# The element-wise part of a long convolution beside attention: smaller steps, another share between two engines, and softmax sums finished in pairs

## The chip, the cores and the metric

One core of a Trainium2 chip runs the whole program in one launch. The metric is device time in microseconds: 3267.9, the median of three runs (3264.78 to 3273.39). The engines are TensorE (PE, with its weight loads as PEld), VectorE (DVE), ScalarE (ACT), GpSimd (POOL) and the DMA queues, of which SyncE (SP) issues most. Each engine has a queue of its own and works it off in order.

## The reference

Two layers of a trunk over 1024 latent tokens (x) and 256 context tokens, 1024 wide. Each layer norms and modulates its input, projects it, and feeds three mixers side by side: attention of 8 heads, a Fourier mixing and a long convolution. The output projection and a squared-ReLU MLP follow. In the second layer the context only gives keys and values. What the change touches is the softmax of the attention and the convolution by FFT:

```python
def block(qs):
    s = einsum('bqhd,bkhd->bhqk', qn, k_nope) + einsum('bqhr,bkr->bhqk', qr, k_rope)
    prob = jax.nn.softmax(s * scale, axis=-1)
    return einsum('bhqk,bkhd->bqhd', prob, v)
...
z = x1 * v
zf = jnp.fft.rfft(z, n=2 * L, axis=1)
kf = jnp.fft.rfft(k, n=2 * L, axis=0)
y = jnp.fft.irfft(zf * kf[None], n=2 * L, axis=1)[:, :L] + d_bias * z
return x0 * y
```

## The kernel before, in words

Every float32 product is made of three matmuls over a high and a low part (`mm3`, lines 138 to 140). The parts come from a copy on ScalarE and a subtraction on VectorE or GpSimd (`split_ps`, lines 143 and 144, from PSUM; `split_sb`, lines 147 and 148, in SBUF).

`attention` walks over 8 heads and, in each, over pairs of query tiles of 128 tokens (`q2`; 4 pairs, and in layer 0 a fifth for the context, which reads only the 256 context keys). For a pair it makes scores against the latent keys (`sx`, 1024 columns, one PSUM tile for each query tile) and the context keys (`se`, both tiles in one bank). Per tile follow: the maximum on VectorE (L1004; L1001 for both tiles' `se`), the bias of the exponential (L1005; L1007 for the context pair), two exponentials on ScalarE that also give their sums (L1008, L1010), the sum of the two sums (L1011) and its reciprocal (L1012; L1015 for the context pair) on VectorE, and the multiplication of the tile `p` by it on GpSimd (L1017). One pair later `turn` transposes `p` on TensorE (L1038, tail L1046), the result `pst` is split into `pt`, and `values` multiplies it with the values (L1056, L1057); `ot` (L1061, L1062) adds the halves. Scores are made two pairs ahead.

Beside it runs `side_job` as a generator: each call of `tick` (one per query tile) advances it by a rate, 0.88 turns in layer 0 and 0.72 in layer 1. Its `hyena_apply` transposes and transforms z on TensorE into `X` (L507, `psz`), then does the element-wise part for both halves `bt` of the frequencies: `zcb` (4 combinations of 512 columns, L535), `zf` (8 of 256, L543), the product with the filter's spectrum (`yf`, `ym`, L552 to L557, 1024 columns), `uq` (8 of 256, L569), `uu` (8 of 256, L577) and the splits `uhl`. Even-numbered combinations go to VectorE, odd ones to GpSimd. TensorE then transforms back (`psy`), and `dz` (L596, L598) is finished. In layer 0 a short second stream for the context follows, without the combinations.

The order in the queues isn't the order of these calls: a scheduler places the recorded instructions on each engine when the program is built. So a generator's step says when something is offered, and the order in the queue has to be read from the built program.

Of the kernel before, what the change touches and what calls it, by code (L numbers as in the profile page):

```python
# [47 lines left out]
def trunk(tc, a):  # L48
# [3 lines left out]
    with ExitStack() as top:  # L52
# [119 lines left out]
        def first_modulation(psp):  # L172
            """scale of the first norm of layer 0, both streams, on TensorE"""
# [36 lines left out]
        def rstd_diag(acc, n, dim, dg):  # L210
            """1 / sqrt(mean + eps) of each token, acc summed over its partitions, on diagonals of 128 tokens"""
# [10 lines left out]
        def rstd_rows(dg, n, r=None):  # L222
            """what rstd_diag found as rows, the same in every partition"""
# [23 lines left out]
        def norm_gen(l, i, xT, c0, c1, hs, acc, dg):  # L247
            """hi and lo parts hs of the modulated norm of tokens c0 to c1, acc filled by sums_by; dg is room"""
# [20 lines left out]
        def final_sums(acc, xs, ps):  # L269
            """as sums_by, the sums over the partitions in every row of ps"""  # L270
# [32 lines left out]
        def new_h(pool, chunks):  # L303
            """tiles for a norm's result: (start, end, hi and lo parts, what is still to run before their use)"""
# [11 lines left out]
        def sine_layers(pool, psp):  # L316
            """the filters' two sine layers, of both model layers and both lengths, to DRAM"""
# [27 lines left out]
        def filters(l, pool, psp):  # L345
            """the long filters' spectra of layer l, to DRAM"""
# [138 lines left out]
        def hyena_apply(l, stream, pool, psp):  # L485
# [35 lines left out]
            for ct in range(2):  # L521
# [4 lines left out]
                dz.append(dzt)  # L526
            Us = []
            for bt in range(2):
# [3 lines left out]
                else:  # L532
                    cb = b8("zcb").rearrange("p (k c f) -> p k c f", k=4, c=2)
                    for i, (p, q, op) in enumerate(((0, 2, ALU.add), (0, 2, ALU.subtract), (1, 3, ALU.add), (1, 3, ALU.subtract))):
                        (G if i % 2 else V).tensor_tensor(cb[:, i].rearrange("p c f -> p (c f)"), x[:, p].rearrange("p c f -> p (c f)"),  # L535
                                        x[:, q].rearrange("p c f -> p (c f)"), op=op)
                    yield
                    zf = b8("zf").rearrange("p (c f n) -> p c f n", c=2, f=4)
                    for c, f, i, ic, j, jc, op in ((0, 0, 0, 0, 2, 0, ALU.add), (0, 1, 0, 0, 2, 0, ALU.subtract),
                                                   (0, 2, 1, 0, 3, 1, ALU.subtract), (0, 3, 1, 0, 3, 1, ALU.add),  # L540
                                                   (1, 0, 0, 1, 2, 1, ALU.add), (1, 1, 2, 1, 0, 1, ALU.subtract),
                                                   (1, 2, 1, 1, 3, 0, ALU.add), (1, 3, 3, 0, 1, 1, ALU.subtract)):
# [10 lines left out]
                G.tensor_tensor(tc_, zs, ks, op=ALU.mult)  # L553
                V.tensor_tensor(yc, yc, tc_, op=ALU.subtract)
                G.tensor_tensor(ys, zc, ks, op=ALU.mult)
                G.tensor_tensor(ts_, zs, kc, op=ALU.mult)
                V.tensor_tensor(ys, ys, ts_, op=ALU.add)  # L557
# [5 lines left out]
                else:  # L563
                    y4 = y.rearrange("p (c f n) -> p c f n", c=2, f=4)
                    q = b8("uq").rearrange("p (k f) -> p k f", k=8)
                    for i, (c, f, g, op) in enumerate(((0, 0, 1, ALU.add), (0, 0, 1, ALU.subtract), (0, 2, 3, ALU.add),
                                                       (0, 3, 2, ALU.subtract), (1, 0, 1, ALU.subtract), (1, 0, 1, ALU.add),
                                                       (1, 2, 3, ALU.add), (1, 2, 3, ALU.subtract))):
                        (G if i % 2 else V).tensor_tensor(q[:, i, :], y4[:, c, f, :], y4[:, c, g, :], op=op)  # L569
                    A_, Ap, B_, H_, E_, Ep, D_, G_ = range(8)  # L570
                    yield
                    u = b8("uu").rearrange("p (r c f) -> p r c f", r=4, c=2)
                    for r, c, i, j, op in ((0, 0, A_, B_, ALU.add), (2, 0, A_, B_, ALU.subtract),
                                           (1, 0, Ap, D_, ALU.add), (3, 0, Ap, D_, ALU.subtract),
                                           (0, 1, E_, G_, ALU.add), (2, 1, E_, G_, ALU.subtract),
                                           (1, 1, Ep, H_, ALU.add), (3, 1, Ep, H_, ALU.subtract)):
                        (G if r % 2 else V).tensor_tensor(u[:, r, c, :], q[:, i, :], q[:, j, :], op=op)  # L577
                    yield
# [4 lines left out]
                yield  # L583
            for _ in range(3):
                yield
# [18 lines left out]
        def fnet(fs, pool, psp, with_ctx):  # L604
            """Fourier mixing, channels and then positions. Channels k of 1 to 31 of each group come with 64 - k, which hold
# [368 lines left out]
        def attention(l, heads, room, hpool, pools, psp, first):  # L974
# [5 lines left out]
            def scores(h, q2, i):  # L980
# [19 lines left out]
                if i == 0:  # L1000
                    V.reduce_max(sm, se, axis=AX.X)  # L1001
# [572 lines left out]
```

## Time and profile before

| what | value |
|---|---|
| median of three runs | 3267.9 us |
| profiled execution, first to last instruction | 3268.1 us |
| attention, layer 0 | about 396 to 772 us |
| attention, layer 1 | about 2081 to 2415 us |
| busy: PE, DVE, ACT, POOL | 95%, 56%, 37%, 32% |
| mean granted clock of TensorE | 0.978 |

The page gives no time around the span, so the span is taken as the profiled execution's own time. The two attention stages make up some 710 us of it; the rest is projections and MLP, with three matmuls per product one after another. A busy share is an average over a stretch: the table of stretches in the section of rows below shows the stages apart.

### The profile page before, as it was taken

Reading aid. Unit: us, or ns where it says so; the run is one execution under the profiler, and the core shown is the slowest. Engines: PE = TensorE matmul, PEld = TensorE weight load, DVE = VectorE, ACT = ScalarE, POOL = GpSimd, SP = SyncE. Lnnn points to the kernel's source line nnn. Section 1 sums busy time; section 2 is a strip of 40 time slices with the busy share of each in tenths; the row PEclk is TensorE's granted clock in tenths of the full one; section 3 lists DMA queues with packets and bytes.
Section 4 is the critical chain, followed back from the end, with each engine's and each line's share of the span. In section 5 each row is a group of like instructions: output and inputs, shape, how many; then the busy total and the mean of one; then the engine's idle time right before and its main releaser. Section 6 shows DMA issues by size and latency. Waiting matters only on the chain. (4 is left out here: it accounts for less than half of the span.)

```text
span 3268.1 us, 41676 instructions
## 1 busy us (share of the span) xinstructions
PE 3096.4 (95%) x16238; PEld 2584.0 (79%) x16238; DVE 1830.7 (56%) x2943; ACT 1204.9 (37%) x2167; POOL 1049.0 (32%) x676
## 2 busy tenths in 40 slices
PE   5999998999999999999999999998998999999997
PEld 1787886887778888888887887787877788888886
DVE  7985679886664444332226535779867322222226
ACT  4324475674331112112214424576654222222113
POOL 6334337542411111111113224347434222222223
PEclk8999998999999999999999998999999999999999
DMA  6454662434222232221113224653242111111113
GB/s 238 157 187 120 200 179 80 128 91 148 84 72 84 91 103 91 78 71 38 35 39 123 94 86 131 218 135 81 68 166 90 39 52 46 46 51 46 51 47 110
DMA packets 121036, 326.29 MB, mean 100 GB/s; under 512 B 32838, under 2 KB 44263, under 8 KB 120584
## 3 DMA queue, kind: packets, MB, share of 16 engines
q1 hardware_dynamic: 107832, 281.88, 27.7%
q0 software_dynamic: 9504, 34.67, 3.5%
q10 hardware_dynamic: 3504, 7.08, 0.6%
q8 instruction: 128, 2.10, 0.3%
q14 instruction: 68, 0.56, 0.1%
HBM read 270.11 MB, written 53.48 MB: 99 GB/s over the span
## 5 line engine op out<-in xcount | busy, mean ns | idle before, releaser
L134 POOL TENSOR_TENSOR wl<-wr,wh 128x1024 fp32r<-128x1024 f32 (+1 forms) x214 | 519.2, 2427 | 1641.8 <-ACT wh L133 1623.9
L133 ACT CAST wh<-wr 128x1024 fp32r<-128x1024 f32 (+1 forms) x214 | 221.5, 1035 | 962.0 <-PE pso L139 680.2
L140 PE MATMUL pso<-uh,wl 128*128 128x512 f32 (+1 forms) x1312 | 484.1, 369 | 4.2 <-POOL wl L134 4.2
L138 PE MATMUL pso<-uh,wh 128*128 128x512 f32 (+1 forms) x1312 | 487.5, 372 | 0.6 <-ACT wh L133 0.6
L1117 DVE SCALAR_TENSOR_TENSOR xT<-pso,modc,xT 128x512 f32<-128x512 f32 (+1 forms) x336 | 241.8, 722 | 438.4 <-PE pso L140 438.4
L138 PE MATMUL psm<-hh,wh 128*128 128x512 f32 (+1 forms) x1280 | 477.4, 374 | 4.3 <-ACT hh L244 4.2
L139 PE MATMUL pso<-ul,wh 128*128 128x512 f32 (+1 forms) x1312 | 480.7, 366 | 0.0
L140 PE MATMUL psm<-hh,wl 128*128 128x512 f32 (+1 forms) x1280 | 472.9, 370 | 3.5 <-POOL wl L134 3.5
L139 PE MATMUL psm<-hl,wh 128*128 128x512 f32 (+1 forms) x1280 | 474.9, 371 | 0.5 <-DVE hl L245 0.4
L1180 DVE SCALAR_TENSOR_TENSOR rl<-psm,rl 128x256 f32<-128x256 f32 (+1 forms) x160 | 101.7, 636 | 460.0 <-ACT rl L1179 459.9
L140 PEld LDWEIGHTS pso<-uh,wl 128*128 128x128 f32 x1312 | 247.8, 189 | 51.5 <-POOL wl L134 5.1
L139 PEld LDWEIGHTS pso<-ul,wh 128*128 128x128 f32 x1312 | 249.5, 190 | 45.2 <-issue 0.5
L138 PEld LDWEIGHTS pso<-uh,wh 128*128 128x128 f32 x1312 | 248.0, 189 | 44.5 <-ACT wh L133 0.8
L138 PEld LDWEIGHTS psm<-hh,wh 128*128 128x128 f32 x1280 | 241.7, 189 | 49.0 <-ACT hh L244 6.5
L140 PEld LDWEIGHTS psm<-hh,wl 128*128 128x128 f32 x1280 | 241.5, 189 | 47.9 <-POOL wl L134 3.9
L139 PEld LDWEIGHTS psm<-hl,wh 128*128 128x128 f32 x1280 | 241.6, 189 | 43.9 <-DVE hl L245 2.5
L1017 POOL TENSOR_SCALAR p<-p,st 128x1280 f32<-128x1280 f32 (+1 forms) x144 | 182.8, 1269 | 268.0 <-DVE st L1012 122.4
L144 DVE TENSOR_TENSOR pt<-pst,pt 128x512 fp32r<-128x512 f32 x328 | 214.4, 680 | 11.7 <-ACT pt L143 10.5
L143 ACT CAST pt<-pst 128x512 fp32r<-128x512 f32 x328 | 181.8, 589 | 86.3 <-PE pst L1038 68.2
L139 PE MATMUL psi<-hl,wh 128*128 128x512 f32 (+1 forms) x536 | 198.4, 370 | 5.8 <-POOL hl L241 3.4
L138 PE MATMUL psi<-hh,wh 128*128 128x512 f32 (+1 forms) x536 | 200.9, 376 | 1.8 <-ACT hh L244 1.1
L140 PE MATMUL psi<-hh,wl 128*128 128x512 f32 (+1 forms) x536 | 197.2, 368 | 3.2 <-POOL wl L134 3.2
(338 smaller groups left out, 6121.0 us busy)
## 6 DMA issues: line engine op xcount, KB each, us to landing
wr<-w SPq DMA_DIRECT2D x144, 512.0 KB, 3.5
wr<-wmod SPq DMA_DIRECT2D x64, 512.0 KB, 3.3
tb<-ftab POOLq DMA_DIRECT2D x34, 512.0 KB, 4.7
wm<-wmod SPq DMA_DIRECT2D x32, 512.0 KB, 3.6
wr<-wout SPq DMA_DIRECT2D x32, 512.0 KB, 3.6
wr<-win SPq DMA_DIRECT2D x26, 512.0 KB, 3.3
d_qk<-qk SPq DMA_DIRECT2D x18, 640.0 KB, 5.3
qk<-d_qk SPq DMA_DIRECT2D x18, 640.0 KB, 6.2
```

Of the source, the lines that this page charges most:

```text
L133: S.copy(hi[:, :n], t[:, :n])
L134: G.tensor_tensor(lo[:, :n], t[:, :n], hi[:, :n].bitcast(F32), op=ALU.subtract)
L138: T.matmul(ps, lhsT=lh, rhs=rh, start=first, stop=False)
L139: T.matmul(ps, lhsT=lh, rhs=rl, start=False, stop=False)
L140: T.matmul(ps, lhsT=ll, rhs=rh, start=False, stop=last)
L143: S.copy(hi, ps)
L144: V.tensor_tensor(lo, ps, hi.bitcast(F32), op=ALU.subtract)
L1017: G.tensor_scalar(pr, pr, st[:, 5:6], 1.0, op0=ALU.mult, op1=ALU.mult)
L1117: V.scalar_tensor_tensor(x, ps[:, : c1 - c0], g, x, op0=ALU.mult, op1=ALU.add)
L1180: V.scalar_tensor_tensor(r[:, :n], ps[:, :n], 0.0, r[:, :n], op0=ALU.max, op1=ALU.mult)
```

## The change

The generator's element-wise part yields after smaller pieces, and a helper `several` decides the engine: the first of every `per` combinations goes to VectorE, the others to GpSimd. `per` is 2 for `zcb` and 4 for `zf`, `uq` and `uu`. The product yields three times more. The order in which `uu` is listed changes. The waiting turns after the part go. The rates rise to 1.1 and 1.0. In the attention the maximum, bias and sums of a pair lie in two small tiles, and `normalise` adds and inverts both tiles' sums in one instruction each, after the second tile's exponentials; the two multiplications on GpSimd follow one another. Docstrings are dropped.

```diff
+            def several(ops, per):
+                for n, (o, x, y, op) in enumerate(ops):
+                    (V if n % per == 0 else G).tensor_tensor(o, x, y, op=op)
+                    if n % per == per - 1:
+                        yield
...
-                        (G if i % 2 else V).tensor_tensor(cb[:, i]..., x[:, p]..., x[:, q]..., op=op)
-                    yield
+                    yield from several([(flat(cb[:, i]), flat(x[:, p]), flat(x[:, q]), op) ...], 2)
...
-                        (G if f % 2 else V).tensor_tensor(zf[:, c, f, :], cb[:, i, ic, :], cb[:, j, jc, :], op=op)
+                    yield from several([(zf[:, c, f, :], cb[:, i, ic, :], cb[:, j, jc, :], op) ...], 4)
...
                 V.tensor_tensor(yc, zc, kc, op=ALU.mult)
                 G.tensor_tensor(tc_, zs, ks, op=ALU.mult)
+                yield
                 V.tensor_tensor(yc, yc, tc_, op=ALU.subtract)
                 G.tensor_tensor(ys, zc, ks, op=ALU.mult)
+                yield
                 G.tensor_tensor(ts_, zs, kc, op=ALU.mult)
+                yield
                 V.tensor_tensor(ys, ys, ts_, op=ALU.add)
...
-                        (G if i % 2 else V).tensor_tensor(q[:, i, :], y4[:, c, f, :], y4[:, c, g, :], op=op)
+                    yield from several([(q[:, i, :], y4[:, c, f, :], y4[:, c, g, :], op) ...], 4)
-                        (G if r % 2 else V).tensor_tensor(u[:, r, c, :], q[:, i, :], q[:, j, :], op=op)
+                    yield from several([(u[:, r, c, :], q[:, i, :], q[:, j, :], op) ...], 4)
...
                         split_sb(uh[:, r], ul[:, r], u[:, r], G)
+                        if r == 1:
+                            yield
                 Us.append((uh, ul))
-                yield
-            for _ in range(3):
                 yield
...
-                    V.tensor_tensor(st[:, 4:5], st[:, 2:3], st[:, 3:4], op=ALU.add)
-                    V.reciprocal(st[:, 5:6], st[:, 4:5])
-                G.tensor_scalar(pr, pr, st[:, 5:6], 1.0, op0=ALU.mult, op1=ALU.mult)
+            def normalise(p, q2):
+                s = p["s"]
+                if q2 < 4:
+                    V.tensor_tensor(s[:, :, 0], s[:, :, 0], s[:, :, 1], op=ALU.add)
+                V.reciprocal(s[:, :, 2], s[:, :, 0])
+                for i in range(2):
+                    G.tensor_scalar(p[i][1], p[i][1], s[:, i, 2:3], 1.0, op0=ALU.mult, op1=ALU.mult)
...
+                scores(pairs[n], h, q2, i)
                 tick()
+                exps(pairs[n], q2, i)
+                if i == 1:
+                    normalise(pairs[n], q2)
...
-                    spawn(0.72 if last else 0.88, side_job(l, psp, xctx, xT, rctx, raw))
+                    spawn(1.0 if last else 1.1, side_job(l, psp, xctx, xT, rctx, raw))
```

GpSimd's queue in layer 0, from the second product of the first half of the frequencies, before (`p` is a normalisation, `x2` two in a row):

```order
L556 TENSOR_TENSOR ym<-zf,wr 128x1024
L1017 TENSOR_SCALAR p<-p,st 128x1280
L148 TENSOR_TENSOR v<-wr,v 128x10x64
L569 TENSOR_TENSOR uq<-yf 128x256
L1017 TENSOR_SCALAR p<-p,st 128x1280
L569 TENSOR_TENSOR uq<-yf 128x256
L1017 TENSOR_SCALAR p<-p,st 128x1280
L569 TENSOR_TENSOR uq<-yf 128x256
L1017 TENSOR_SCALAR p<-p,st 128x1280
L569 TENSOR_TENSOR uq<-yf 128x256
L577 TENSOR_TENSOR uu<-uq 128x256 x4
L1017 TENSOR_SCALAR p<-p,st 128x1280
```

The same place after the change, from the context pair's two normalisations on (L530 is the line in `several`, L558 and L563 are the products, L1025 is the normalisation):

```order
L1025 TENSOR_SCALAR p<-p,st 128x256 x2
L558 TENSOR_TENSOR ym<-zf,wr 128x1024
L563 TENSOR_TENSOR ym<-zf,wr 128x1024
L310 DMA tb<-itab 128x1024
L530 TENSOR_TENSOR uq<-yf 128x256 x6
L530 TENSOR_TENSOR uu<-uq 128x256 x3
L1025 TENSOR_SCALAR p<-p,st 128x1280 x2
L530 TENSOR_TENSOR uu<-uq 128x256 x3
L148 TENSOR_TENSOR v<-wr,v 128x10x64
L1025 TENSOR_SCALAR p<-p,st 128x1280 x2
```

Normalisations, which stood singly between one or a few combinations, now stand in twos, with two products and nine combinations between one pair's and the next.

VectorE's queue in layer 0, from the last sum of the product on (L557), before:

```order
L557 TENSOR_TENSOR yf<-yf,ym 128x1024
L1012 RECIPROCAL st<-st 128x1
L144 TENSOR_TENSOR pt<-pst,pt 128x512
L1005 SCALAR_TENSOR_TENSOR st<-st,sm,acol 128x1
L144 TENSOR_TENSOR pt<-pst,pt 128x4x128
L569 TENSOR_TENSOR uq<-yf 128x256 x4
L1011 TENSOR_TENSOR st<-st 128x1
L1001 TENSOR_REDUCE sm<-se 128x2
L1012 RECIPROCAL st<-st 128x1
L1062 TENSOR_TENSOR ot<-ot,pv 64x256
```

The same place after the change (L565 is that sum; L1010 and L1004 are maxima, L1011 the bias, L1022 and L1023 the sum and the reciprocal for both tiles):

```order
L565 TENSOR_TENSOR yf<-yf,ym 128x1024
L1011 SCALAR_TENSOR_TENSOR sm<-sm,acol 128x1
L1069 TENSOR_TENSOR ot<-ot,pv 64x256
L1010 TENSOR_REDUCE sm<-sx 128x1
L1004 TENSOR_REDUCE sm<-se 128x2
L1022 TENSOR_TENSOR st<-st 128x2
L530 TENSOR_TENSOR uq<-yf 128x256
L1023 RECIPROCAL st<-st 128x2
L1011 SCALAR_TENSOR_TENSOR sm<-sm,acol 128x1
L144 TENSOR_TENSOR pt<-pst,pt 128x512
L1010 TENSOR_REDUCE sm<-sx 128x1
L530 TENSOR_TENSOR uq<-yf 128x256
```

Four `uq` in a row have become single ones among the attention's instructions, and one addition and one reciprocal serve both tiles of a pair.

## Rows read from the trace of the kernel before

**Rows 1.** The page's first part: busy us, share and instructions per engine.
```profile
PE 3096.4 (95%) x16238; PEld 2584.0 (79%) x16238; DVE 1830.7 (56%) x2943; ACT 1204.9 (37%) x2167; POOL 1049.0 (32%) x676
```

**Rows 2.** Stretches: length, busy us (instructions) of PE, PEld, DVE, ACT, POOL; clock, DMA.
```profile
493.00:594.30 101.30, 80.21 (x459) 69.00 (x458) 95.02 (x155) 56.83 (x121) 74.56 (x63) 0.85 0.26 67
690.00:760.00 70.00, 64.30 (x441) 56.01 (x440) 56.81 (x125) 51.92 (x114) 27.64 (x22) 1.00 0.48 158
2100.00:2201.00 101.00, 97.58 (x696) 88.19 (x695) 77.91 (x163) 77.26 (x161) 41.65 (x38) 1.00 0.52 134
2201.80:2317.60 115.80, 100.31 (x639) 85.06 (x638) 110.95 (x195) 79.50 (x167) 79.07 (x61) 0.96 0.29 72
```

**Rows 3.** Waits of TensorE, 493 to 594.3 us: total us, times, longest.
```profile
PE pv L1056 <- DVE pt L144: 7.4, 6, 2.9
```

**Rows 4.** Groups of VectorE, 493 to 594.3 us: busy us, mean ns | idle before.
```profile
L1005 DVE SCALAR_TENSOR_TENSOR st<-st,sm,acol 128x1 f32<-128x1 f32 x14 | 10.7, 766 | 0.1
L543 DVE TENSOR_TENSOR zf<-zcb 128x256 f32<-128x256 f32 x8 | 7.6, 984 | 0.1
L569 DVE TENSOR_TENSOR uq<-yf 128x256 f32<-128x256 f32 x8 | 6.8, 908 | 0.0
...
L1011 DVE TENSOR_TENSOR st<-st 128x1 f32<-128x1 f32 x15 | 5.7, 383 | 0.1
...
L577 DVE TENSOR_TENSOR uu<-uq 128x256 f32<-128x256 f32 x8 | 4.2, 567 | 0.0
...
L1012 DVE RECIPROCAL st<-st 128x1 f32<-128x1 f32 x15 | 2.2, 149 | 0.0
```

**Rows 5.** Groups of VectorE, 2201.8 to 2317.6 us.
```profile
L1005 DVE SCALAR_TENSOR_TENSOR st<-st,sm,acol 128x1 f32<-128x1 f32 x22 | 12.0, 547 | 0.0
L1011 DVE TENSOR_TENSOR st<-st 128x1 f32<-128x1 f32 x23 | 10.3, 449 | 2.7 <-ACT p L1010 2.5
...
L543 DVE TENSOR_TENSOR zf<-zcb 128x256 f32<-128x256 f32 x5 | 5.2, 1073 | 0.0
L577 DVE TENSOR_TENSOR uu<-uq 128x256 f32<-128x256 f32 x8 | 4.9, 646 | 0.0
...
L569 DVE TENSOR_TENSOR uq<-yf 128x256 f32<-128x256 f32 x8 | 4.5, 576 | 0.0
```

**Rows 6.** Groups of VectorE, 690 to 760 us (calm).
```profile
L1005 DVE SCALAR_TENSOR_TENSOR st<-st,sm,acol 128x1 f32<-128x1 f32 x15 | 4.2, 279 | 0.0
...
L1012 DVE RECIPROCAL st<-st 128x1 f32<-128x1 f32 x16 | 2.5, 156 | 0.1
L1011 DVE TENSOR_TENSOR st<-st 128x1 f32<-128x1 f32 x16 | 2.4, 152 | 4.5 <-ACT p L1010 4.4
```

**Rows 7.** Groups of GpSimd, 493 to 594.3 us.
```profile
L543 POOL TENSOR_TENSOR zf<-zcb 128x256 f32<-128x256 f32 x8 | 7.4, 951 | 0.1
L569 POOL TENSOR_TENSOR uq<-yf 128x256 f32<-128x256 f32 x8 | 6.9, 877 | 8.1 <-DVE st L1012 5.7 <-DVE st L1011 2.4
L577 POOL TENSOR_TENSOR uu<-uq 128x256 f32<-128x256 f32 x8 | 6.4, 819 | 1.1 <-DVE st L1011 1.1
L556 POOL TENSOR_TENSOR ym<-zf,wr 128x1024 f32<-128x1024 f32 x2 | 4.7, 2373 | 0.0
```

**Rows 8.** Timeline of VectorE: start us, us, engine, line, instruction.
```profile
499.83 1.92 DVE L1005 SCALAR_TENSOR_TENSOR st<-st,sm,acol 128x1 f32<-128x1 f32 x1
```

**Rows 9.** Timeline of GpSimd at the same time.
```profile
499.38 2.35 POOL L555 TENSOR_TENSOR yf<-zf,wr 128x1024 f32<-128x1024 f32 x1
```

**Rows 10.** Timeline of GpSimd, 2117 to 2125 us (calm).
```profile
2118.74 1.33 POOL L1017 TENSOR_SCALAR p<-p,st 128x1280 f32<-128x1280 f32 x1 [3.83 <-DVE st L1012]
2122.30 1.33 POOL L1017 TENSOR_SCALAR p<-p,st 128x1280 f32<-128x1280 f32 x1 [2.22 <-DVE st L1012]
```

**Rows 11.** Timeline of TensorE, the transposes of the first of these tiles.
```profile
2128.32 1.03 PE L1038 MATMUL pst<-ident,p 128*128 128x128 f32 x8
```

**Rows 12.** Waits of the whole run: VectorE's additions for an exponential's sum.
```profile
DVE st L1011 <- ACT p L1010: 59.8, 41, 4.0
```

More of the change, by code (lines that the diff above doesn't have):

```diff
@@ L581, in hyena_apply @@
                         split_sb(uh[:, r], ul[:, r], u[:, r], G)
+                        if r == 1:
+                            yield
                 Us.append((uh, ul))
-                yield
-            for _ in range(3):
                 yield
@@ L1009, in scores @@
-                if isx:
-                    S.activation(P[:, :SEQ], sx, AF.Exp, bias=st[:, 1:2], scale=ac, accum_out=st[:, 3:4])
-                    V.tensor_tensor(st[:, 4:5], st[:, 2:3], st[:, 3:4], op=ALU.add)
-                    V.reciprocal(st[:, 5:6], st[:, 4:5])
-                    pr = P
-                else:
-                    V.reciprocal(st[:, 5:6], st[:, 2:3])
-                    pr = P[:, SEQ:TT]
-                G.tensor_scalar(pr, pr, st[:, 5:6], 1.0, op0=ALU.mult, op1=ALU.mult)
@@ L1018, in scores @@
-                yield P
+                me, mx, b = (m[:, 2 * u + i : 2 * u + i + 1] for u in range(3))
+                if q2 < 4:
+                    V.reduce_max(mx, p["x", i], axis=AX.X)
+                    V.scalar_tensor_tensor(b, mx, me, nac, op0=ALU.max, op1=ALU.mult)
+                else:
+                    V.tensor_tensor(b, me, nac, op=ALU.mult)
+                S.activation(P[:, SEQ:TT], p["e"][:, i, :], AF.Exp, bias=b, scale=ac, accum_out=s[:, i, 0:1])
+                if q2 < 4:
+                    S.activation(P[:, :SEQ], p["x", i], AF.Exp, bias=b, scale=ac, accum_out=s[:, i, 1:2])
@@ L1063, in values, with emit @@
                 nc.sync.dma_start(out=d_cat[h // 2][mine, q2 * 256 : q2 * 256 + 256], in_=ot[mine])
-            units = [(h, q2, i) for h in range(HEADS) for q2 in range(nq2) for i in range(2)]
-            ready = {}
-            def emit_scores(n):
-                if n >= len(units):
+            todo = [(h, q2) for h in range(HEADS) for q2 in range(nq2)]
+            pairs = [{} for _ in todo]
+            def emit(n, i):
+                if n >= len(todo):
                     return
-                h, q2, i = units[n]
+                h, q2 = todo[n]
                 if q2 == 1 and i == 0 and h + 1 < HEADS:
@@ L1075, in emit_scores @@
                     split_v(h + 1, heads)
-                g = scores(h, q2, i)
-                next(g)
-                pending.append((n, g))
+                scores(pairs[n], h, q2, i)
                 tick()
-            pending = []
-            def softmaxes():
-                while pending:
-                    n, g = pending.pop(0)
-                    ready[n] = next(g)
+                exps(pairs[n], q2, i)
+                if i == 1:
+                    normalise(pairs[n], q2)
             for _ in range(2):
                 next(first)
-            for n in range(4):
-                emit_scores(n)
-                softmaxes()
-                if n == 1:
+            for n in range(2):
+                for i in range(2):
+                    emit(n, i)
+                if n == 0:
                     split_v(0, heads)
@@ L1096, in attention @@
                     spawn(1.0, first)
-            prev = []
-            for n in range(0, len(units), 2):
-                h, q2, _ = units[n]
+            for n, (h, q2) in enumerate(todo):
+                P = [pairs[n][i][0] for i in range(2)]
                 dst = [ptile(4) for _ in range(2)] if q2 < 4 else []
-                turn(ready[n], 0, dst)
-                emit_scores(n + 4)
-                softmaxes()
-                turn(ready[n + 1], 1, dst)
-                tail = turn_tail([ready.pop(n), ready.pop(n + 1)])
-                emit_scores(n + 5)
-                softmaxes()
+                turn(P[0], 0, dst)
+                emit(n + 2, 0)
+                turn(P[1], 1, dst)
+                tail = turn_tail(P)
+                emit(n + 2, 1)
                 pts = [(4 * b + u, dst[b][0][:, u], dst[b][1][:, u]) for b in range(len(dst)) for u in range(4)]
```

60 lines of the change are left out of this document (27 added, 33 removed).

## Prediction

> **What bounds the kernel now.** I read the page's table of engines first: TensorE is busy for 95% of the span, VectorE for 56%, GpSimd for 32% [rows 1]. An average like that hides stages, so next came the busy time by stretch [rows 2]. All that the change touches runs during the attention of the two layers, and there two stretches stand out. From 493.0 to 594.3 us (layer 0; called A) and from 2201.8 to 2317.6 us (layer 1; called B) the long convolution's element-wise part runs. In A VectorE is busy 95.02 of 101.30 us, TensorE only 80.21, at a granted clock of 0.85; in B VectorE 110.95 of 115.80, TensorE 100.31, at 0.96. In the two calm stretches beside them TensorE is idle 5.7 of 70 us and 3.4 of 101 us at full clock. So in A and B VectorE is the bound, elsewhere TensorE. The waits of TensorE in A agree: the longest one in total is for the second half of the split of transposed probabilities, which VectorE does late [rows 3].
>
> How much is there to win? Matmuls issued are a fair measure of progress, since the mix is nearly the same: 441 in the 70 us of the layer 0 calm stretch, that is 6.30 a us. A's 459 matmuls would take 72.9 us at that pace, B's 639 would take 101.4: 28.4 and 14.4 us are lost, 42.8 together. By the pace of the other calm stretch (696 in 101 us, more short ones) B loses 23.1. So 43 to 52 us is the most that mending A and B can give.
>
> **The change, part by part.**
>
> *Twelve 256-wide combinations per layer go from VectorE to GpSimd.* Before, each of three groups (zf, uq, uu) has eight, four on either engine, for two halves of the frequencies: 24 on VectorE. Now two of eight stay: 12 leave VectorE. In A the three groups hold eight each at 984, 908 and 567 ns [rows 4]; four of each are 4 x (0.984 + 0.908 + 0.567) = 9.8 us. In B they take 1073, 576 and 646 ns [rows 5], so 4 x 2.295 = 9.2 us. The zcb group and the products keep their engines. These durations hold waiting time (next point but one), so they are what VectorE gets back only if the waiting goes as well.
>
> *Sums finished for two query tiles together.* Per pair of tiles with all 1280 keys, one addition and one reciprocal go. The new ones are two elements wide instead of one; no row shows that width. It lies between free and twice the price of the 128x1 ones, which cost 152 and 156 ns when nothing disturbs them [rows 6]; twice would be 0.31 us a pair, 6 us in A and B together. I take free, since 152 ns for a single element is nearly all fixed cost. In A the addition takes 383 and the reciprocal 149 ns [rows 4]; with 7.5 pairs that is 4.0 us. In B it is (0.449 + 0.149) x 11 = 6.6 us [rows 4, 5]. Outside A and B about 52 pairs save 0.31 us each [rows 6], 16 us of VectorE; TensorE is the bound there, so between 0 and 16 of it shows. I take 4, near the low end, since TensorE's idle share in the calm stretches is only 3 to 8%.
>
> *What GpSimd gains.* It takes 12 more combinations per layer: in A at the mean of 951, 877 and 819 ns, 10.6 us more on a queue that is busy 74.56 of 101.30 us [rows 2, 7]. That is where the price is. A VectorE instruction with one element per partition (L1005, the bias of the exponential) took 1.92 us at 499.83 and ended together with GpSimd's multiplication yf, which ran from 499.38 for 2.35 us [rows 8, 9]. Its mean is 766 ns in A, 547 in B and 279 in the calm stretch [rows 4 to 6], while the reciprocal, which reads one tensor, stays at 149 to 156. The Trainium skill ("SBUF — State Buffer", section "Who interferes with whom") states this as a rule: a VectorE instruction with two SBUF inputs contends with a GpSimd instruction that reads SBUF, and whichever starts first blocks the other for the whole instruction. The trace agrees, 1.92 us against 0.28. By that rule taken whole, every combination handed to GpSimd becomes a lock of its own, and the sum is that of rival 1; by the price below, it is the forecast's.
>
> Price: in A the excess of L1005 is 14 x (0.766 - 0.279) = 6.8 us, that of the half of L1011 that remains 7.5 x (0.383 - 0.152) = 1.7. GpSimd's share would rise from 0.74 to (74.6 + 10.6) / 91 = 0.94, by a factor 1.27, so 2.3 us are added. The element-wise instructions left on VectorE pay a like sum (estimate: the same again), 4.5 in all. In B: 5.9 + 3.3 = 9.2 us of excess, share 0.68 to 0.84, 2.2 added, doubled 4.4. Bounds: nothing added (the instructions at risk are also fewer), or each of the 12 moved instructions blocks VectorE for its whole 0.7 to 0.9 us, 10 us a layer.
>
> *Normalisation later.* The first tile's multiplication now waits for the second tile's sums. In a calm place of layer 1 the two multiplications stand at 2118.74 and 2122.30, and the first tile is transposed from 2128.32 (the layer's ninth multiplication and ninth group of eight transposes) [rows 10, 11]. So the delay of 3.6 us eats into a lead of 8.25 and leaves 4.7: hidden. In the first pair of each layer there is hardly a lead; I charge 1 us for both. In A the cover is thin. In GpSimd's queue two multiplications ym, six uq and three uu now stand between one pair's normalisation and the next: 2 x 2.37 + 6 x 0.88 + 3 x 0.82 = 12.5 us [rows 7], against a pair's 8 to 9 in calm. Before, one or two combinations stood between normalisations there.
>
> *Small steps, higher rates, fewer waiting turns.* The generator now yields some 28 times where it yielded 15, at a rate of 1.1 for 0.88 (1.0 for 0.72 in layer 1). But in the finished order the part still spans nine or ten pairs on GpSimd's queue in layer 0 (8.5 before) and ten in layer 1 (11 before): it is not spread out. What the steps do is break up bursts of four uq or uu on VectorE. I count nothing for that. TensorE's inverse transforms move a few pairs later; their work is the same, and they lie in stretches where TensorE is the bound: 0. The loads on SP's queue shift with the steps, and none is on TensorE's path in A or B: 0.
>
> **Sum.** A: 9.8 + 4.0 - 4.5 = 9.3 us. B: 9.2 + 6.6 - 4.4 = 11.4. Outside 4, start -1. Together 24 us off the profiled execution's 3268.1 (0.2 above the median of the timed runs): 3244. After that VectorE is at about 86 of 92 us in A: still the bound, so the relief shows in full; GpSimd is close behind.
>
> **Rivals.**
> 1. GpSimd takes VectorE's place. For: the 12.5 us piece, a share of 0.94 in A, and L1005 held until yf ends. Against: GpSimd idles 26.7 us in A now, 8.1 of it before uq alone, waiting for VectorE [rows 7]. If each of the 24 moved instructions blocks VectorE for as long as it runs (10.6 + 8.8 us), 19.0 of element-wise relief becomes nothing; 10.6 of sums remain, less 5 for normalisations that come late: 3262.
> 2. The whole loss goes. For: once VectorE falls below TensorE, idling and the lower clock (0.85 in A) go together. Against: VectorE stays the longer one in A by my sum. 43 to 52 us: 3221.
> 3. Slower: the one sum left blocks VectorE's queue. In the whole run VectorE waits 59.8 us in 41 places for an exponential's sum before an addition [rows 12], 1.46 each, with reductions and splits queued behind. There are now 64 additions, each behind the later of two exponentials. If all 64 wait for 1.46 us, that is 93, or 34 more, and if TensorE feels it all, 24 won turn into 10 lost: 3278. It decides from 1.46 us per addition on. Against: the addition now comes once a pair, so there are half as many chances, and in calm stretches VectorE has slack.
>
> **How the numbers follow.** The forecast, 12 to 36 us won (3232 to 3256), gets 0.53; rival 1 (0 to 12 won) 0.21; rival 2 (over 36) 0.15; rival 3 and anything else that loses 0.11. Less than 0.3% (9.8 us) is about what a measurement can't tell from no change. Faster by more: 0.53 + 0.15 + a little of rival 1 = 0.70; same 0.20; slower 0.10. The range 3218 to 3270 leaves out the far end of rival 2 and most of rival 3.
>
> **What would show it.** Right: in the element-wise stretches VectorE's share falls below 94%, TensorE's clock comes back near 1.00, pairs take some 10% less; zf, uq and uu on VectorE 12 per layer; 64 additions and 72 reciprocals. Wrong: L1005's successor above 0.8 us with the stretches as long as now (rival 1); TensorE's transposes waiting for GpSimd's p (rival 1); VectorE waiting over 90 us for exponentials (rival 3); or gains in calm stretches, where I expect next to none.

## The result and the profile after

| kernel | median us | range | runs | ratio to before |
|---|---|---|---|---|
| before | 3267.99 | 3264.78 to 3274.76 | 5 | |
| changed | 3287.99 | 3282.57 to 3302.93 | 5 | 1.0066 [1.0048, 1.0084] |

The change makes the kernel slower by 20 us, 0.66%. The forecast was 24 us faster, so sign and range are both wrong. The execution that was profiled is the slowest of the five (span 3301.0 us; the others reach down to 3280.6), so it is read by progress inside a stretch (matmuls issued in it), not by its end.

The engine table of the page after, against [rows 1]: VectorE has 160 instructions less and 10.2 us less work, GpSimd 24 more and 23.8 us more, TensorE the same.

```profile
PE 3096.2 (94%) x16238; PEld 2581.6 (78%) x16238; DVE 1820.5 (55%) x2783; ACT 1205.7 (37%) x2167; POOL 1072.8 (32%) x700
```

Where the time goes is in the stretches. First three of the kernel before, cut by content this time: the whole element-wise part of layer 0 (from the first `zcb` to the last `uhl`), that of layer 1, and 100 us that hold the inverse transforms of layer 0. Columns as in [rows 2].

```profile
480.70:588.20 107.50, 88.37 (x532) 76.73 (x530) 100.38 (x162) 62.33 (x131) 77.05 (x65) 0.87 0.35 87
2178.80:2305.90 127.10, 112.42 (x740) 97.60 (x740) 120.79 (x211) 86.81 (x181) 88.31 (x73) 0.96 0.36 87
600.00:700.00 100.00, 96.21 (x668) 86.00 (x667) 80.25 (x167) 69.24 (x148) 49.61 (x48) 0.98 0.50 132
```

The same three after the change:

```profile
479.20:586.60 107.40, 83.92 (x531) 72.90 (x529) 89.36 (x134) 65.05 (x138) 85.31 (x78) 0.90 0.37 89
2186.60:2308.70 122.10, 104.83 (x677) 91.23 (x675) 111.09 (x161) 81.41 (x169) 94.86 (x81) 0.93 0.34 84
620.00:720.00 100.00, 86.15 (x582) 78.15 (x581) 65.23 (x122) 56.03 (x119) 41.77 (x43) 0.93 0.47 120
```

Three findings. In layer 0 VectorE has 11.0 us less to do (9.3 were forecast), and nothing comes of it: 531 matmuls in 107.4 us against 532 in 107.5. VectorE now idles 18 us where it idled 7. In layer 1, 677 matmuls at the pace of before (740 in 127.1) would take 116.3 us; they take 122.1: 5.8 lost. In the inverse transforms, 582 at the pace of before (668 in 100) would take 87.1; they take 100: 12.9 lost. Together that is 18.7 us, an estimate from matmul counts. Whole attentions of the same execution, from the first score matmul to the last `ot`, took 395.0 us instead of 375.6 in layer 0 and 340.4 instead of 337.1 in layer 1, so part of layer 1's 5.8 is won back outside its stretch. Of the 32.9 us that this span is longer than the one before, 8.8 lie ahead of the first attention, which the change doesn't touch.

The relief in layer 0 turns into this. VectorE in the changed kernel (start, us, line; L557 and L560 are the product and the subtraction of `yf`):

```profile
493.17 1.74 DVE L557 TENSOR_TENSOR yf<-zf,wr 128x1024 f32<-128x1024 f32 x1 [1.32 <-POOL zf L530]
501.76 3.35 DVE L560 TENSOR_TENSOR yf<-yf,ym 128x1024 f32<-128x1024 f32 x1 [6.84 <-POOL ym L558]
505.14 0.42 DVE L1069 TENSOR_TENSOR ot<-ot,pv 64x256 f32<-64x256 f32 x1
```

GpSimd at the same time:

```profile
490.45 5.76 POOL L530 TENSOR_TENSOR zf<-zcb 128x256 f32<-128x256 f32 x6
496.18 2.33 POOL L561 TENSOR_TENSOR yf<-zf,wr 128x1024 f32<-128x1024 f32 x1
498.49 0.93 POOL L1025 TENSOR_SCALAR p<-p,st 128x256 f32<-128x256 f32 x2
499.40 2.33 POOL L558 TENSOR_TENSOR ym<-zf,wr 128x1024 f32<-128x1024 f32 x1
501.69 2.33 POOL L563 TENSOR_TENSOR ym<-zf,wr 128x1024 f32<-128x1024 f32 x1
```

And TensorE:

```profile
505.71 1.94 PE L1045 MATMUL pst<-ident,p 128*128 128x128 f32 x8 [9.44 <-DVE ot L1069]
```

VectorE wants `ym`, which stands behind six `zf` in a row, another product and two normalisations: 6.84 us of waiting. Then the subtraction itself takes 3.35 us instead of 1.2, since GpSimd starts the next `ym` 0.07 us ahead of it. The `ot` behind it comes late, and TensorE stands for 9.44 us. Much of the price that the forecast spread over many instructions is paid in one place. In the group means of the whole element-wise part of layer 0, against [rows 4], the bias is better than before (463 ns, it was 766). The paired addition is not: 767 ns where a single one took 383, so eight cost 6.1 us where fifteen cost 5.7. Over the whole run its median is 161 ns (152 in [rows 6] for the single one), so it isn't the second element that costs.

```profile
L1011 DVE SCALAR_TENSOR_TENSOR sm<-sm,acol 128x1 f32<-128x1 f32 x15 | 6.9, 463 | 0.0
L1022 DVE TENSOR_TENSOR st<-st 128x2 f32<-128x2 f32 x8 | 6.1, 767 | 2.1 <-ACT p L1016 2.0
...
L560 DVE TENSOR_TENSOR yf<-yf,ym 128x1024 f32<-128x1024 f32 x2 | 4.5, 2273 | 6.8 <-POOL ym L558 6.8
```

In layer 1 the same place shows another face. One bias of 128x1 lasts 7.16 us:

```profile
2209.45 7.16 DVE L1011 SCALAR_TENSOR_TENSOR sm<-sm,acol 128x1 f32<-128x1 f32 x1
```

GpSimd runs without a gap until 2216.59, 0.02 us before that bias ends:

```profile
2207.86 2.63 POOL L1025 TENSOR_SCALAR p<-p,st 128x1280 f32<-128x1280 f32 x2
2210.47 1.53 POOL L148 TENSOR_TENSOR v<-wr,v 128x640 fp32r<-128x640 f32 x1
2211.97 2.33 POOL L558 TENSOR_TENSOR ym<-zf,wr 128x1024 f32<-128x1024 f32 x1
2214.26 2.33 POOL L561 TENSOR_TENSOR yf<-zf,wr 128x1024 f32<-128x1024 f32 x1
```

In the inverse transforms it is a table, a block of coefficients that each group of matmuls needs. TensorE's waits from 600 to 720 us (us in all, times, longest), the first matmuls behind the longest wait, and the stretches ahead of it and behind it:

```profile
PE psy L138 <- DMA tb<-itab: 6.9, 3, 3.9
...
643.99 0.58 PE L138 MATMUL psy<-tb,uhl 128*128 128x256 f32 x1 [3.91 <-DMA tb<-itab]
644.37 0.41 PE L139 MATMUL psy<-tb,uhl 128*128 128x256 f32 x1
644.58 0.41 PE L140 MATMUL psy<-tb,uhl 128*128 128x256 f32 x1
...
630.00:640.00 10.00, 9.74 (x77) 8.86 (x76) 7.28 (x17) 6.74 (x16) 6.22 (x7) 1.00 0.50 119
644.00:648.00 4.00, 4.00 (x19) 4.00 (x19) 0.70 (x1) 0.00 (x0) 1.17 (x1) 0.50 0.12 39
```

After the idle 3.9 us the matmuls start 0.21 us apart where those ahead of the wait (from 638.41) started 0.12 apart. The granted clock is 0.50 from 644 to 648 us, the lower of its two levels (1.2 of 2.4 GHz), so the wait is paid a second time. The tables are requested from GpSimd's queue. The one of the longest wait was requested at 637.07, directly behind two normalisations, and TensorE went on 6.9 us later. Ahead of the next requests GpSimd's queue stood for 4.39 us until TensorE gave a buffer back:

```profile
634.48 2.67 POOL L1025 TENSOR_SCALAR p<-p,st 128x1280 f32<-128x1280 f32 x2 [1.47 <-DVE st L1023]
637.07 0.60 POOL L310 DMA_DIRECT2D tb<-itab  x1
...
652.02 1.25 POOL L310 DMA_DIRECT2D tb<-itab  x2 [4.39 <-PE psy L140]
```

### The profile page after: what moved, and what is told of

The parts are those of the page before. It is cut to its first block, busy times and chain, and to the rows that moved or that the text cites. A ratio compares the mean times of both kernels' runs of the same rounds, so it can differ in the third digit from the quotient of the medians.

```text
span 3301.0 us, 41509 instructions
## 1 busy us (share of the span) xinstructions
PE 3096.2 (94%) x16238; PEld 2581.6 (78%) x16238; DVE 1820.5 (55%) x2783; ACT 1205.7 (37%) x2167; POOL 1072.8 (32%) x700
## 4 chain that ended last, share of the span: by engine, by line
PE 71%; DVE 15%; ACT 4%; POOL 4%; issue 3%; DMA 2%; SPq 0%; ACTq 0%; POOLq 0%; DVEq 0%
PE pso L138 9%; PE pso L140 9%; PE pso L139 9%; PE psm L138 8%; PE psm L139 8%; PE psm L140 8%; DVE pt L144 3%; PE psi L138 3%; PE psi L140 3%; PE psi L139 3%; DVE sm L1010 2%; PE pv L1063 1%; PE pv L1064 1%; ACT p L1016 1%; DVE crow L201 1%
## 5 line engine op out<-in xcount | busy, mean ns | idle before, releaser
L1025 POOL TENSOR_SCALAR p<-p,st 128x1280 f32<-128x1280 f32 (+1 forms) x144 | 180.4, 1264 | 269.6 <-DVE st L1023 198.4
```

The lines of the kernel that those rows point to most:

```text
L1025: G.tensor_scalar(p[i][1], p[i][1], s[:, i, 2:3], 1.0, op0=ALU.mult, op1=ALU.mult)
```

## The experiments

All ratios are to the kernel before; each variant was timed 5 to 12 times. Three theories: the split makes VectorE and the normalisations wait for GpSimd (1); the sums for two tiles bring the normalisation late (2); the steps and the rate move the inverse transforms to where they collide (3).

**One part at a time.** `c_pair_only` is before with the paired sums, `a_split_only` before with three of four combinations on GpSimd, `bc_half` the changed kernel with the old half split, `ab_no_pair` the changed kernel with the old attention.

```diff
# a_split_only, on before
-(G if f % 2 else V).tensor_tensor(zf...)
+(V if f == 0 else G).tensor_tensor(zf...)      # uq and uu alike
# bc_half, on the changed kernel
-(V if n % per == 0 else G).tensor_tensor(o, x, y, op=op)
+(V if n % 2 == 0 else G).tensor_tensor(o, x, y, op=op)
```

Expected of c_pair_only: 

> The kernel before with the sums of two query tiles finished together and nothing else: engines, steps and rates of the element-wise part are those of before. Theory 1 (the split of three to one makes VectorE's queue and the normalisations wait for GpSimd): the pairing is harmless, 3255 to 3268 us, 0 to 13 faster than before. Theory 2 (the pairing brings each first tile's normalisation too late): 3280 to 3288, the whole loss. Theory 3 (steps and rates put the inverse transforms where they collide with other work): as before, 3262 to 3270.

Expected of a_split_only: 

> The kernel before with three of four of the 256-wide combinations on GpSimd (uu in the listing order of before), steps, rates and sums as before. Theory 1: slower, 3278 to 3290, with TensorE waiting over 10 us for GpSimd's normalisations. Theory 2 and theory 3: not slower, 3255 to 3268, since VectorE is relieved of 12 instructions a layer.

Expected of bc_half: 

> The changed kernel with every second combination back on VectorE; small steps, rates and paired sums stay. Theory 1: the loss goes, 3255 to 3268. Theory 2 and theory 3: the loss stays, 3280 to 3290.

Expected of ab_no_pair: 

> The changed kernel with the sums and normalisations tile by tile as before; the split of three to one, the small steps and the rates stay. Theory 1: the loss stays or grows, 3285 to 3300. Theory 2: the loss goes, 3255 to 3268. Theory 3: the loss stays, 3280 to 3295.

Measured: sums alone 1.0011 [1.0002, 1.0020], split alone 0.9989 [0.9977, 1.0001], all but the split 1.0038 [1.0024, 1.0052], all but the sums 1.0044 [1.0031, 1.0057]. Each of the two that hold steps and rate loses most of the 0.66%; the two parts that my sum was made of do little alone (3264.7 us for the split, 3271.5 for the sums), so theories 1 and 2 are refuted as the whole cause. Theory 3 leads, but the parts don't add up.

The trace shows where the sums alone cost. In `c_pair_only` TensorE waits 12.9 us in 7 places for `p`; in the attentions of the kernel before it has no wait for GpSimd's `p`. The longest is in layer 0's element-wise part, where both normalisations stand behind the products in GpSimd's queue:

```profile
547.62 2.33 POOL L556 TENSOR_TENSOR ym<-zf,wr 128x1024 f32<-128x1024 f32 x1
549.94 2.64 POOL L1021 TENSOR_SCALAR p<-p,st 128x1280 f32<-128x1280 f32 x2
...
551.32 1.11 PE L1041 MATMUL pst<-ident,p 128*128 128x128 f32 x4 [8.14 <-POOL p L1021]
```

**Steps or rate?** Steps take the turns from 15 to 28 and the rates rise from 0.88 to 1.1 (0.72 to 1.0), so the transforms, whose turns are as before, run faster. A rate that changes between the two parts separates them.

```diff
# after_oldpace, on the changed kernel; before_newpace likewise on before
+ pace["c"] = spawn(0.72 if last else 0.88, ...)              # from the start (1.0, 1.1)
+ pace["c"][1] = 1.34 if l == DEPTH - 1 else 1.64   # ahead of the element-wise part (0.536, 0.59)
+ pace["c"][1] = 0.72 if l == DEPTH - 1 else 0.88   # ahead of the inverse transforms (1.0, 1.1)
# abc_byresult, on the changed kernel
-G.tensor_tensor(tc_, zs, ks, op=ALU.mult)
+V.tensor_tensor(tc_, zs, ks, op=ALU.mult)
-V.tensor_tensor(ys, ys, ts_, op=ALU.add)
+G.tensor_tensor(ys, ys, ts_, op=ALU.add)
```

Expected of after_oldpace: 

> The changed kernel with the timetable of the kernel before: the rate is 0.88 (0.72 in layer 1) in the transforms and 1.64 (1.34) in the element-wise part, so that its more numerous turns take as many ticks as the old ones; small steps, 3:1 split and paired sums stay. Theory 3a (the rate is what costs: the inverse transforms come too fast, their tables and spectra arrive late): 3262 to 3274, TensorE's wait of psy for the table tb below 3 us, attention of layer 0 back below 785 us. Theory 3b (the small steps and the split themselves cost, VectorE waits on GpSimd's ym and the probabilities are multiplied late): 3280 to 3290, the wait of pst for p stays at 12 or more.

Expected of before_newpace: 

> The kernel before with the timetable of the changed one: rate 1.1 (1.0) in the transforms and 0.59 (0.536) in the element-wise part, so that its fifteen turns take as many ticks as the new ones; nothing else is changed. Theory 3a (the rate): 3274 to 3284, with psy waiting for the table tb 5 us or more and the loss in the stretch of the inverse transforms of layer 0. Theory 3b (steps and split): 3263 to 3271, no measurable change.

Expected of steps_half_oldpace: 

> The kernel before with the small steps only: VectorE and GpSimd still take every second combination, the sums are not paired, and the timetable is the old one (0.88 and 0.72 in the transforms, 1.64 and 1.34 in the element-wise part). Half split with small steps and pairing had lost least in the element-wise stretch of layer 0. Theory 3a: 3245 to 3262, a gain that the higher rate had hidden. Theory 3b: 3270 to 3280.

Expected of abc_byresult: 

> The changed kernel, with the product's four multiplications and two additions dealt out by result: all that makes yc on VectorE, all that makes ys on GpSimd, three each as before four and two, so that VectorE never waits there for GpSimd's ym. If VectorE's wait for ym (6.8 us in one place, TensorE idle 9.4 behind it) is a cause, 3278 to 3283 and no wait of TensorE over 6 us near 500 us; if the rate alone is the cause, 3285 to 3292.

Measured: after_oldpace 3274.1, 1.0024 [1.0014, 1.0033]; before_newpace 3275.8, 1.0024 [1.0015, 1.0032]; steps_half_oldpace 1.0013 [1.0003, 1.0024]; abc_byresult 3289.3, 1.0066 [1.0053, 1.0080]. The rate alone, put on the kernel before, costs 0.24%, and by the mechanism named: TensorE's waits there, 600 to 720 us,

```profile
PE psy L139 <- DMA tb<-itab: 8.0, 3, 5.4
```

against 2.5 us in the whole run before. The other way round, the old timetable takes 0.42 of the 0.66% off the changed kernel; there `psy` still waits 5.5 us for tables, 1.8 of it in layer 0, where under 3 had been expected. The steps bring no gain that the rate had hidden; that hope fell. `abc_byresult` took VectorE's wait for `ym` away and won nothing: instead one bias took 7.75 us. VectorE:

```profile
494.51 7.75 DVE L1011 SCALAR_TENSOR_TENSOR sm<-sm,acol 128x1 f32<-128x1 f32 x1
```

GpSimd, whose run ends at 502.24, the bias at 502.26:

```profile
493.73 2.38 POOL L565 TENSOR_TENSOR yf<-yf,ym 128x1024 f32<-128x1024 f32 x1
496.06 4.14 POOL L530 TENSOR_TENSOR uq<-yf 128x256 f32<-128x256 f32 x6
500.16 2.08 POOL L530 TENSOR_TENSOR uu<-uq 128x256 f32<-128x256 f32 x3
```

**Where the rate costs, and what a run on GpSimd does.** On the changed kernel: the old rate in the inverse transforms alone; its own rate, but the tables requested one pair ahead into buffers that are free by then; the old timetable in the context's stream too; GpSimd's runs broken up.

```diff
# after_inv_oldpace
+ if R == 4: pace["c"][1] = 0.72 if l == DEPTH - 1 else 0.88   # back to 1.0, 1.1 after the inverse
# after_tables_early
-for r in range(R):
-    tb = [load_tab("itab", r, bt, pool)... for bt in range(2)]
+nxt = itabs(0)              # odd r: both tables in one b8 buffer
+for r in range(R):
+    tb, nxt = nxt, itabs(r + 1) if r + 1 < R else None
# after_gap
+ if n % per: G.memset(o[:, :1], 0.0)      # and behind each product on G
```

Expected of after_inv_oldpace: 

> The changed kernel at its own rate (1.1 and 1.0) but for the latent stream's inverse transforms, which go at the old 0.88 and 0.72. If the inverse transforms of layer 0 are where the rate costs (psy waiting for its tables, about 20 us lost in that stretch against 5 before), 3272 to 3280 and psy's wait for tb below 3 us. If the rate costs in the forward transforms and at the start of the element-wise part, 3283 to 3290.

Expected of after_tables_early: 

> The changed kernel at its own rate, with the second and the fourth pair of inverse tables in one of the big buffers that are free by then, and each pair requested before the pair ahead of it is used; three table buffers made GpSimd's queue stand at a table's request until TensorE had finished with a buffer. If the tables' late arrival is the mechanism in the inverse transforms: no wait of psy for a table over 1 us, 3272 to 3281. If the tables are only a sign and the fast transforms themselves crowd the pairs: 3284 to 3290.

Expected of after_oldpace2: 

> As after_oldpace, but the context's stream of layer 0 is put on the old timetable too (0.98 in its part of ten turns that had nine); in after_oldpace it ended a pair later than before and 6.7 us were lost in one pair near the end of the layer, against 1.7 before. If that pair was an artefact of the late end: 3266 to 3271, and what is left of the change costs at most 0.1%. If steps, split and sums themselves cost the rest: 3272 to 3276 as there.

Expected of after_gap: 

> The changed kernel with a one-column fill on GpSimd after nearly every combination and product there (it zeroes one column of each result, so the output is not the reference's). GpSimd's unbroken runs of six to nine combinations are so broken into ones and twos. In the changed kernel one 128x1 instruction on VectorE (the bias) took 7.16 us in layer 1 and ended with such a run. If a run as a whole holds VectorE: no 128x1 instruction on VectorE over 3 us, attention of layer 1 some 5 us shorter, 3279 to 3286. If VectorE is held by each GpSimd instruction alone and 7.16 us was something else: one over 4 us stays, and the time is 3286 to 3293.

Measured: after_inv_oldpace 3275.1, 1.0031 [1.0015, 1.0047]; after_tables_early 3278.5, 1.0039 [1.0027, 1.0051]; after_oldpace2 3276.2, 1.0033 [1.0021, 1.0046]; after_gap 3289.2, 1.0075 [1.0062, 1.0089]. Tables that come early take 0.27 of the 0.66% away at the changed kernel's own rate. `psy` waits for no table any more, and its stretch of inverse transforms is at 657 matmuls in 100 us (582 after, 668 before):

```profile
610.00:710.00 100.00, 93.45 (x657) 83.76 (x656) 78.10 (x144) 67.97 (x145) 45.69 (x43) 0.98 0.42 109
```

So in the inverse transforms the late tables are what the rate costs. The idea of an artefact in the context's stream fell. `after_gap` stays open: the 7.16 us in layer 1 went and its attention, from the first copy of `ot` to the last, took 312.8 us instead of 316.8, but in layer 0 two `ym` still ran together and held a bias for 5.20 us, TensorE's longest wait for `p` rose to 6.7, and in all nothing was won. Time and the one hold over 4 us fit the second theory of its expectation, but that theory has no place for a hold over two instructions.

**Why the rest doesn't add up.**

```diff
# split_late_only, on before: zf stays half and half, uq and uu go 3:1
# split_and_sums = a_split_only with the changed attention; split_late_and_sums = split_late_only with it
# steps_split_oldpace2 = after_oldpace2 with the old attention
# tables_early_zf_half = after_tables_early with zf half and half
# split_late_l0 = split_late_only, in layer 0 alone
-(G if i % 2 else V).tensor_tensor(q[:, i, :]...)
+(G if i % (2 if l == DEPTH - 1 else 4) else V).tensor_tensor(q[:, i, :]...)   # uu alike
```

Expected of split_and_sums: 

> The kernel before with the 3:1 split and the paired sums, without small steps and at the old rate. If the effects add up (-0.11% and +0.11%): ratio 0.999 to 1.001. If the split turns into a loss beside the sums, because both multiplications of a pair then stand behind GpSimd's longer runs: 1.0015 to 1.004, with pst waiting for p 9 us or more.

Expected of steps_split_oldpace2: 

> The changed kernel without the paired sums, with the old timetable in both streams: small steps and 3:1 split. If the effects add up (+0.13% and -0.11%): ratio 0.999 to 1.001. If the split turns into a loss beside the steps, because the steps offer all six zf of a half to GpSimd ahead of the product: 1.0015 to 1.003, and VectorE waits over 4 us for ym in one place.

Expected of split_late_only: 

> The kernel before with the 3:1 split of uq and uu only; zf stays half and half, so that GpSimd reaches the product after four combinations as before. If the run of zf is what hurts the split, this keeps the gain and loses the harm: ratio 0.995 to 0.9985, the best so far. If relief and harm go together wherever the combinations are: 0.998 to 1.0005, as the whole split.

Expected of tables_early_zf_half: 

> The changed kernel with the tables requested early (1.0039 of before) and zf split half and half again, so that GpSimd's run ahead of the product has four combinations instead of six. If VectorE's standing behind that run is the rest of the loss: 1.001 to 1.0025 and no DVE instruction or wait over 5 us in the first half of the element-wise part. If not: 1.003 to 1.0045.

Expected of split_late_and_sums: 

> The kernel before with the paired sums and the 3:1 split of uq and uu only (zf half and half). If the split and the sums collide at the six zf ahead of the product: ratio 1.000 to 1.002, near the sum of the two alone (0.9993 and 1.0011). If they collide wherever combinations stand ahead of a pair's two multiplications (products and uq run 11 us in one piece there): 1.003 to 1.0045, as with the whole split.

Expected of split_late_l0: 

> The kernel before with the 3:1 split of uq and uu in layer 0 alone; layer 1, the steps, the rates and the sums stay as before. In split_late_only the attention of layer 0 took 339 us against 350 and that of layer 1 314 against 313. If that is the split's doing: 3255 to 3262, ratio 0.996 to 0.999. If it was chance of one execution: 0.999 to 1.001.

| kernel | median us | ratio |
|---|---|---|
| split_and_sums | 3278.6 | 1.0042 [1.0026, 1.0058] |
| split_late_and_sums | 3268.8 | 1.0011 [1.0000, 1.0023] |
| steps_split_oldpace2 | 3275.0 | 1.0018 [1.0007, 1.0028] |
| split_late_only | 3264.7 | 0.9993 [0.9981, 1.0005] |
| tables_early_zf_half | 3275.5 | 1.0031 [1.0019, 1.0043] |
| split_late_l0 | 3258.9 | 0.9982 [0.9969, 0.9994] |

Split and sums, a small gain and a small loss, make 0.42% together, without any step or rate. With `zf` left half and half the same pair costs 0.11%, the sums' own price. So they collide at the six `zf` ahead of the product. VectorE's waits in the whole run of split_and_sums name it:

```profile
DVE yf L554 <- POOL ym L553: 10.1, 2, 5.2
```

The split alone has one such wait of 2.3 us, and in split_late_and_sums none is over 1.1. GpSimd's timeline in split_and_sums shows what stands ahead of `ym` in layer 0:

```profile
488.87 3.17 POOL L543 TENSOR_TENSOR zf<-zcb 128x256 f32<-128x256 f32 x4
492.02 3.62 POOL L1021 TENSOR_SCALAR p<-p,st 128x1280 f32<-128x1280 f32 x2
495.60 1.42 POOL L543 TENSOR_TENSOR zf<-zcb 128x256 f32<-128x256 f32 x2
496.97 2.38 POOL L555 TENSOR_TENSOR yf<-zf,wr 128x1024 f32<-128x1024 f32 x1
499.31 2.34 POOL L553 TENSOR_TENSOR ym<-zf,wr 128x1024 f32<-128x1024 f32 x1
```

Both normalisations of a pair now come in one piece, and here they fall among the six `zf` ahead of the product; with the split alone they stood singly, both ahead of the `zf`, and VectorE still had maxima and a split of the attention to do meanwhile. The other wait is in layer 1, behind six `zf` in one run without a normalisation among them:

```profile
2198.75 5.64 POOL L543 TENSOR_TENSOR zf<-zcb 128x256 f32<-128x256 f32 x6
...
2209.65 3.35 DVE L554 TENSOR_TENSOR yf<-yf,ym 128x1024 f32<-128x1024 f32 x1 [5.25 <-POOL ym L553]
```

In the changed kernel with mended tables, `zf` half and half gave only 1.0031 for 1.0039, within the intervals. VectorE's wait for `ym` fell there from 6.8 to 2.2 us, and the subtraction behind it lasted 5.65 us instead of 3.35. What is left, 0.31%, is near what the steps (0.13) and the sums (0.11) cost alone; this I have not shown further. Whether the split adds to the steps (0.18 measured, 0.02 by addition) the intervals leave open; the wait for `ym` of over 4 us that was expected there did not come, it is 2.3.

The version that the traces point to, the late split in layer 0 only, beats both kernels: 0.9982 of before, 7 us (2 to 10 by the interval), with every other part of the change left out. (`split_late_only`, in both layers, was hoped to be at 0.9985 or below and came to 0.9993.) In the profiled executions, one of each kernel, the split's gain lies in layer 0: its attention took 368.1 us in `a_split_only`, 365.3 in `split_late_only` and 367.6 in `split_late_l0`, against 375.6 before. Layer 1's took 339.5, 338.2 and 337.3 against 337.1. With the sums beside the whole split (`split_and_sums`) the gain is gone: 377.0 and 344.1.

## Why the prediction was wrong

The runs with one part each price the sum's terms. The split was worth 10.1 us in it (9.8 and 9.2 less 4.5 and 4.4); alone it won some 4, with 0 inside the interval. The paired sums were worth 13.6 (4.0, 6.6 and 4 less 1); alone they lost some 4. Together the two lost some 14, which no term had. Steps, rate and loads stood at 0; the rate alone lost some 8, the steps alone some 4.

**Twelve combinations off VectorE: right in size, wrong in worth.** Twelve a layer went, VectorE's work in layer 0's part fell by 11.0 us (9.8 and 4.0 less a price were counted). The failed step is "After that VectorE is at about 86 of 92 us in A: still the bound, so the relief shows in full". In the changed kernel the instructions behind a waiting one wait too (the `ot` at 505.14). With GpSimd's share of the part grown from 77 to 85 us, the relief became waiting for `ym`. That VectorE's subtraction and its addition in each product need GpSimd's results was in the code, and the sum had no term for it.

**"So the delay of 3.6 us eats into a lead of 8.25 and leaves 4.7: hidden", with 1 us charged: failed.** The lead was read in a calm place. In `c_pair_only`, which has this part alone, TensorE waits 12.9 us for `p`, 8.14 of it at one place of the element-wise part; the prediction had said of that part only that "the cover is thin".

**The price of 4.5 us a layer: wrong in form.** It was spread over many instructions from their mean excess. Measured: the bias's mean fell to 463 ns in layer 0, the paired addition's rose to 767, and single instructions lasted 3.35 and 7.16 us. So of the 4.0 us that halving the additions and reciprocals was to save in A, the additions' 2.9 did not come. (The "about 52 pairs" outside A and B should be 45 or 46 of the 64; the term of 4 us does not hang on it.)

**"TensorE's inverse transforms move a few pairs later ... they lie in stretches where TensorE is the bound: 0", and "The loads on SP's queue shift with the steps, and none is on TensorE's path in A or B: 0": failed.** The tables go through GpSimd's queue, not SP's, with three buffers for two tables at a time, and at the higher rate `psy` waits for them 6.9 us, after A has ended. Put on the kernel before, the rate costs 0.24% (before_newpace); taken off the changed one, it gives back 0.42% (after_oldpace), and early tables alone give back 0.27%.

**"What the steps do is break up bursts of four ... on VectorE": half right.** On VectorE single ones came; on GpSimd's queue runs of six to nine arose, which I had listed as "12.5 us [rows 7], against a pair's 8 to 9 in calm" and put into the sum at nothing (the 1 us is for the first pair of each layer). But that piece is not where split and sums collide without the steps: `split_late_and_sums` keeps its `uq` and `uu` and costs the sums' own 0.11%. The run of six `zf` ahead of the product does it, and the prediction does not mention that one.

**Rivals.** Rival 1, GpSimd takes VectorE's place, had the mechanism and the wrong price: 3262, since it thought that the relief could only become nothing. Of its two signs the bias above 0.8 us failed (463 ns), and TensorE's waiting for `p` came (12.1 us in 11 places). Rival 3 is refuted: 64 additions and 72 reciprocals, as counted, and VectorE's waits for an exponential's sum are, against [rows 12],

```profile
DVE st L1022 <- ACT p L1016: 57.1, 36, 2.5
```

Rival 2's condition, VectorE below TensorE, didn't arise. Its sign that the clock comes back hardly showed: 0.90 for 0.87 in layer 0's part, and 0.93 for 0.96 in layer 1's. In layer 1's calm stretch, 396 matmuls in 58 us (6.8 a us, 6.9 before), nothing changed, as expected. One sign that the prediction named for being right, VectorE's share below 94%, came true in a slower kernel (83 and 91%): a share also falls when an engine waits.

## What to carry to other kernels

When work moves from one in-order queue to another, count not only the busy time but also the hand-overs: what stands ahead of the first result that the relieved engine wants back, in the new queue's order. A rate or a step that only shifts work also shifts its transfers; look at the queue that issues them and at its buffers before costing it at nothing. Two parts that are each within 0.11% of nothing made 0.42% together, so parts of a change are to be tried in pairs too.

## What the runs showed of the hardware

The surprise is how long a hold can last. In [rows 8, 9] a VectorE instruction was held until one GpSimd instruction ended. In three kernels here the longest bias of 128x1 was held until an unbroken run of GpSimd instructions ended: 7.16 us (run's end 2216.59, bias's end 2216.61), 7.75 us (502.24 and 502.26), 5.20 us in after_gap (two `ym` from 492.40 to 497.06, the bias until 497.08). VectorE didn't get in between two instructions there. The Trainium skill ("SBUF — State Buffer", section "Who interferes with whom") speaks of a block for the whole instruction; these three are blocks over four, ten and two instructions. The 5.20 us began at 491.88, 0.52 us ahead of the first `ym`, while GpSimd issued a table's load.

It isn't the rule. In the kernel before, a bias came free at the end of the first of two `ym`, with the second directly behind:

```profile
555.73 1.99 DVE L1005 SCALAR_TENSOR_TENSOR st<-st,sm,acol 128x1 f32<-128x1 f32 x1
...
555.34 2.37 POOL L553 TENSOR_TENSOR ym<-zf,wr 128x1024 f32<-128x1024 f32 x1
557.67 2.37 POOL L556 TENSOR_TENSOR ym<-zf,wr 128x1024 f32<-128x1024 f32 x1
```

And in the changed kernel, during GpSimd's run of six `zf` (490.45 to 496.21), VectorE's own second `zf` took 0.40 us, and the product behind it ended at 494.91:

```profile
491.44 0.40 DVE L530 TENSOR_TENSOR zf<-zcb 128x256 f32<-128x256 f32 x1
```

What makes the difference, no run tells. After the one of 7.16 us, the longest bias in the changed kernel lasts 1.43 us.
